# An encoder kernel with split-precision matmuls: elementwise work taken from GpSimd, and the mLSTM query prepared one group ahead

## The chip, the cores and the metric

The kernel runs on one core of a Trainium2 chip. The metric is the device time of one execution in microseconds (us): 1479.44 us, the median of 3 runs (1478.56 to 1479.59). One more execution was profiled; the views of the profile below come from it. The engines are TensorE (PE: matmuls, with PEld for the loading of the stationary operand), VectorE (DVE), ScalarE (ACT), GpSimd (POOL) and SyncE (SP), whose queue issues all the DMAs here.

## The reference

A two-layer encoder is applied to a prompt of 1024 tokens (`p`) and to a sample of 512 tokens (`s`), each with 1024 features, in float32. After each layer stands `x = layer_norm(ALPHA * x + mix)`.

Layer 0 (even) is a pool mixer beside a bidirectional mLSTM with 4 heads of 128, computed in chunks of 128 tokens:

```python
proj = x @ w_in; xa, za, xb, vb, ob, zb, gi, gf = jnp.split(proj, IN0_SPLIT_POINTS, axis=-1)
out_a = centred_pool_mixer(xa, w_pool, pool_scale) * silu(za)   # window means of 2, 4, 8, 16, minus x, then w_pool
xc = silu(centred_depthwise_conv(xb, conv_w, conv_b))           # 3 taps
q, k = xc @ w_q, xc @ w_k                                       # per head
# per chunk and direction, g = cumsum(log forget gate):
s = (q @ k.T) * exp(dmat - m_row)          # dmat causal, from the gates
num = s @ v + ex * (C @ q);  den = s.sum(-1) + ex * (n @ q)
h = num / maximum(abs(den), exp(-m_row))
C_new = decay * C + (ws * v).T @ k;  n_new = decay * n + ws @ k
out_b = (head_norm((h_fwd + h_bwd) * sigmoid(ob)) * g + skip * xc) * silu(zb)
mix = concatenate([out_a, out_b]) @ w_out
```

Layer 1 (odd) is attention with 8 query heads and 2 key heads, RMS norm and rotary tables on q and k, a softmax over the whole sequence, and a gate `silu(z)` before the output projection.

## The kernel before, in words

Every large matmul is made of three, with operands split into a high and a low part in float32r: high x high, high x low, low x high. To split a 128x512 tile takes one cast to float32r (the high part) and one subtraction (the low part). The helpers at lines 92 to 103 set the engines: `hi_pool` casts on POOL, `hi_act` on ACT, `lo_dve` subtracts on DVE, and `split_light` casts on ACT and subtracts on POOL. `mm` (line 106) issues one matmul, so most PE rows carry L106, most casts L93 or L96, most low parts L99 or L103.

The work has three stages, which the profile shows at about 0 to 155, 155 to 622, and 622 us to the end.

*First projections* (`layer0`, lines 295 to 337). For each of two pieces of 512 columns (v, then the output gate) and each of three groups of 512 tokens (p0, p1, s0), four accumulators in PSUM (`tp`, `ts`) take 24 matmuls each. ACT evacuates them into `evp` or `evs` (tag `th` of the pool `st0`, 3 buffers; lines 320 to 326) and SP stores them to DRAM. Gate columns are transposed into PSUM banks (`ctpa`, `ctpws`, `ctpex`, `ctpen`, line 507) that the accumulators before them held. Between the groups steps of `weight_sums` (line 1107) run: pieces of layer 1's weights are loaded into tiles `sr` (8 buffers), four subtractions per piece (two on POOL, two on DVE, line 1120) make sums, and these are stored for layer 1.

*Heads* (lines 338 to 404). Six periods: prompt heads 0, 1, 2 and 3 (two groups of 512 tokens each), then sample heads 0 and 1 together, and 2 and 3 together (one group each); so each period has two groups. In a period `merge` interleaves generators by their declared numbers of steps: `chains` (the passing of the state from chunk to chunk) of this period, `early` (convolution, query, scores and chunk sums) of the next, `head_fin` (norm and gating) of the one before, and projections with the pool mixer (`proj_g`, `pool_mix`) as filling. `early(s, h, ...)` (line 551) runs head by head. Per group it makes the convolution `xc` (564 to 569); splits it into `kh`, `kl`; forms q by `wqp` = three matmuls with a product of w_q and w_k, and splits it into `keep`; loads and exponentiates the gate weights `w` (ACT line 603) and masks them on POOL (606); transposes `xc` to `kt`; loads and splits v (`vh`, `vl`); multiplies `S` = k q and weights it into `ph`, `pl` (633 to 636); then twice, for two chunks each, forms `vw` = v times ws on POOL (643), splits it into `vwh`, `vwl`, multiplies `U` (the chunk sums) and `A` (the within-chunk numerators `N`). `kh`, `kl`, `vh`, `vl`, `vw`, `vwh` and `vwl` have one buffer each, q's `keep` has four. In this stage the weights of the projections (`wunit`) are split by `split_light`, since `wlight` is set. `pool_mix` makes the window sums on POOL (817) and casts its result with `hi_pool`. `out_weights` splits every second weight tile of the output projection with `split_light`.

*The rest*: the output projection and layer norm of layer 0 (part of it inside the heads' last periods, `mid_tile`, whose norm ends with two products on POOL at lines 929 and 930), then layer 1.

What sets the order: the program is emitted in the order of the generators, and a scheduler that simulates a timeline orders each engine's queue from it (`TileContext(nc, schedule_with_timeline_sim=True)`); only layer 1's PE order is written out by hand. Engines then run their queues in order. POOL also computes `rstd` as a power (line 195).

## Time and profile before

| | |
|---|---|
| median of 3 runs | 1479.44 us (1478.56 to 1479.59) |
| the profiled execution, its own time | 1477.55 us |
| its span, first to last instruction | 1475.8 us |
| instructions | 21781 |
| mean granted clock of TensorE | 0.990 |
| ACT, busy us | 738.4 (50%) |
| DMA moved, mean rate | 243.42 MB, 165 GB/s |

Engines' busy times are unions of their instructions. A matmul's recorded duration overlaps with the next one's, so matmuls are better counted by the distance of their starts. In a row of groups the fields are: line, engine, operation, tiles (output, then inputs), shapes, count, then busy us and mean ns of one, then the idle time of the engine before them and what ended it. A row of waits reads: engine and tile that waited, line, what released it, total us, times, longest. A row of the timeline or of the chain begins with start and duration in us from the span's start. The granted clock is the share of TensorE's full clock in that stretch.

### The profile page before, as it was taken

The page shows a single profiled execution, that of the slowest core. Times are in us where ns is not written, and L with a number is a line of the kernel's source. Part 1 is how long each engine was busy: PE and PEld are TensorE (multiplying, and loading weights), DVE is VectorE, ACT ScalarE, POOL GpSimd, SP SyncE. Part 2 cuts the span into 40 slices and gives each one's busy share as a digit, 9 for nine tenths or more (in the row PEclk, how much of TensorE's full clock was granted, in tenths as well). Part 3 has the DMA queues.
Part 4 walks back from the last instruction along what each step waited for, and adds up shares of the span by engine and source line. Part 5 has one row for each costly group of instructions (what it writes and reads, how often), then busy time and mean ns, then how long its engine had stood idle before and what let it go on. Part 6 is the DMA issues. An engine that isn't in the chain of part 4 may idle for free.

```text
span 1475.8 us, 21781 instructions
## 1 busy us (share of the span) xinstructions
PE 1435.2 (97%) x7190; PEld 1189.3 (81%) x7190; DVE 1012.5 (69%) x1976; ACT 738.4 (50%) x1666; POOL 609.0 (41%) x616
## 2 busy tenths in 40 slices
PE   9998999999999999999999999999999999999997
PEld 7876888878787788788888789888878888888886
DVE  6584156585777878877779548555677777777675
ACT  3341355454545555445346545557755555555551
POOL 5431334353542333659426002432345545444641
PEclk9998999999999999999999999999999999999999
DMA  9976564555597776545554876345321111111311
GB/s 311 396 282 235 190 201 139 204 176 178 160 310 245 233 229 208 181 147 185 172 167 145 271 226 234 121 136 157 114 72 58 57 51 37 43 58 58 100 51 57
DMA packets 181586, 243.42 MB, mean 165 GB/s; under 512 B 14673, under 2 KB 90193, under 8 KB 181473
## 3 DMA queue, kind: packets, MB, share of 16 engines
q1 hardware_dynamic: 181472, 242.03, 49.7%
q8 instruction: 57, 0.93, 0.3%
q14 instruction: 57, 0.46, 0.1%
HBM read 155.94 MB, written 86.03 MB: 164 GB/s over the span
## 4 chain that ended last, share of the span: by engine, by line
PE 65%; DVE 13%; DMA 12%; issue 4%; ACT 3%; POOL 2%; SPq 1%; DVEq 0%; ACTq 0%; POOLq 0%
PE Sp L106 6%; PE Op L106 6%; PE o1p L106 6%; PE ptp L1442 4%; PE o1s L106 3%; PE qs L106 3%; PE o0s L106 3%; PE z L106 3%; PE zp L106 3%; PE o0p L106 3%; PE xbp L106 2%; PE kvs L106 2%; PE ts L106 1%; PE Ss L106 1%; PE z4P L106 1%
## 5 line engine op out<-in xcount | busy, mean ns | idle before, releaser
L1420 POOL TENSOR_SCALAR prp<-prp,smp 128x1024 f32<-128x1024 f32 x64 | 73.3, 1145 | 137.8 <-DVE smp L1419 112.7
L96 ACT CAST pwp<-ptp 128x512 fp32r<-128x512 f32 x128 | 74.8, 585 | 92.1 <-PE ptp L1442 91.4
L106 PE MATMUL Op<-pwp,Vhp 128*128 128x512 f32 x256 | 109.0, 426 | 0.6 <-DVE pwp L99 0.6
L99 DVE TENSOR_TENSOR pwp<-ptp,pwp 128x512 fp32r<-128x512 f32 x128 | 87.2, 682 | 22.9 <-ACT pwp L96 22.7
L1415 ACT ACTIVATE prp<-Sp,nbp,rqp 128x1024 f32<-128x1024 f32 (+1 forms) x68 | 78.8, 1159 | 21.6 <-DVE nbp L1412 15.8
L1407 DVE TENSOR_REDUCE nbp<-Sp 128x1 f32<-128x1024 f32 (+1 forms) x68 | 78.4, 1153 | 11.8 <-PE Sp L106 11.7
L1442 PEld LDWEIGHTS ptp<-idn,prp 128*128 128x128 f32 x512 | 63.5, 140 | 20.0 <-DVE pwp L99 1.9
L1442 PE MATMUL ptp<-idn,prp 128*128 128x128 f32 x512 | 77.0, 272 | 2.0 <-POOL prp L1420 1.4
L106 PEld LDWEIGHTS Op<-pwp,Vhp 128*128 128x128 f32 x256 | 48.3, 189 | 8.0 <-DVE pwp L99 1.0
L106 PE MATMUL tp<-wt_l,xhp 128*128 128x512 f32 x128 | 51.2, 404 | 0.0
L106 PE MATMUL tp<-wt_h,xlp 128*128 128x512 f32 x128 | 51.1, 403 | 0.0
L106 PE MATMUL o0p<-wo0l,ah0p 128*128 128x512 f32 x128 | 50.8, 399 | 0.2 <-DVE wo0l L99 0.2
L106 PE MATMUL o0p<-wo0h,ah0p 128*128 128x512 f32 x128 | 50.6, 397 | 0.2 <-ACT wo0h L96 0.2
L106 PE MATMUL tp<-wt_h,xhp 128*128 128x512 f32 x128 | 50.7, 403 | 0.0
L106 PE MATMUL o0p<-wo0h,al0p 128*128 128x512 f32 x128 | 50.3, 394 | 0.0
L106 PE MATMUL Op<-pwp,Vlp 128*128 128x512 f32 x128 | 50.1, 391 | 0.0
L1067 POOL TENSOR_TENSOR rskp<-sskp,mhalf 128x2 f32<-128x2 f32 x8 | 7.0, 879 | 100.2 <-DVE sskp L1063 100.2
L106 PE MATMUL Sp<-Khp,qhp 128*128 128x512 f32 x128 | 41.9, 403 | 0.0
L106 PE MATMUL o1p<-wo,ah1p 128*128 128x512 f32 x128 | 40.7, 399 | 0.0
L106 PE MATMUL Sp<-Klp,qhp 128*128 128x512 f32 x128 | 40.7, 393 | 0.0
L106 PE MATMUL Sp<-Khp,qlp 128*128 128x512 f32 x128 | 40.4, 391 | 0.0
L699 DVE SCALAR_TENSOR_TENSOR Usp<-Usp,decbp 128x130 f32<-128x130 f32 x48 | 22.2, 462 | 25.8 <-ACT Usp L656 25.2
(1150 smaller groups left out, 4999.5 us busy)
## 6 DMA issues: line engine op xcount, KB each, us to landing
wt_r<-w0t SPq DMA_DIRECT2D x16, 256.0 KB, 5.2
xrp<-xT_p SPq DMA_DIRECT2D x16, 256.0 KB, 5.4
srq<-w1q SPq DMA_DIRECT2D x16, 256.0 KB, 5.4
sum_q<-srq SPq DMA_DIRECT2D x16, 256.0 KB, 5.3
srz<-w1z SPq DMA_DIRECT2D x16, 256.0 KB, 5.1
sum_z<-srz SPq DMA_DIRECT2D x16, 256.0 KB, 4.8
wp<-rd_p SPq DMA_DIRECT2D x16, 256.0 KB, 4.9
z_p<-zsp SPq DMA_DIRECT2D x16, 256.0 KB, 3.2
```

Source lines behind the costliest of these rows:

```text
L96: self.nc.scalar.copy(out, in_)
L99: self.nc.vector.tensor_tensor(out=out, in0=in_, in1=hi.bitcast(F32), op=ALU.subtract)
L106: self.nc.tensor.matmul(out, lhsT=lhsT, rhs=rhs, start=start, stop=stop)
L699: nc.vector.scalar_tensor_tensor(out=U[:, i, :], in0=U[:, i + o, :], scalar=dec[:, 4 * d + h, n:n + 1], in1=U[:, i, :], op0=ALU.mult, op1= ...
L1067: nc.gpsimd.tensor_tensor(out=rs[:, 0:nh], in0=ss[:, 0:nh], in1=self.mhalf[:, 0:nh], op=ALU.pow)
L1407: nc.vector.tensor_reduce(out=nb[:, i:i + 1], in_=b, op=ALU.max, axis=AX.X, negate=True)
L1415: nc.scalar.activation(pr[:, i * W:(i + 1) * W], b, AF.Exp, bias=nb[:, 0:1], scale=rq, accum_out=sm[:, i:i + 1])
L1420: nc.gpsimd.tensor_scalar(pr, pr, sm, 0.0, ALU.mult, ALU.add)
L1442: nc.tensor.transpose(pt[:, h * P:(h + 1) * P], prs[h][:, c * P:(c + 1) * P], self.idn)
```

## The change

- The evacuation tiles `th` of the first projections get 4 buffers, the tiles `sr` of the weight sums 7 instead of 8; all four subtractions of a piece run on DVE.
- In the heads `wunit` casts on ACT and subtracts on DVE (`hi_w = hi_act`, and `wlight` is never set). `out_weights` does so for all its tiles. The casts of `kh`, `vh` and of the pool mixer go from POOL to ACT; the window sums and the products `vw` go from POOL to DVE. POOL keeps the masks (606), the powers (195), memsets and the layer norm's two products.
- `early` takes all heads of a period as one stream: all convolutions first, then `query` (the split of k, q and its split) for the first group, and for each group, once S is done, `query` of the next group ahead of U and A. The tiles N and keep are taken in `query`. The product `vw` for the first two chunks is made ahead of the step's end at S, the one for the other two right after the first U. The stream is declared with 8 steps a group instead of 10.

The diff, cut to its core:

```diff
@@ -317,7 +317,7 @@
-                            t = st.tile([P, 512], F32, tag="th", name=f"ev{s}{piece}{n}")
+                            t = st.tile([P, 512], F32, tag="th", name=f"ev{s}{piece}{n}", bufs=4)
@@ -343,7 +343,7 @@
-            self.wlight = True
+            self.hi_w = self.hi_act
@@ -388,8 +388,8 @@
-                    jobs.append((chain(*[self.early(*hd, hp, hf) for hd in periods[i + 1]]),
-                                 total(lambda s: 10 * self.seqs[s][0] // 512, periods[i + 1])))
+                    jobs.append((self.early(periods[i + 1], hp, hf),
+                                 total(lambda s: 8 * self.seqs[s][0] // 512, periods[i + 1])))
@@ -401,7 +401,7 @@
-            self.wlight = False
+            self.hi_w = self.hi_pool
@@ -548,51 +548,72 @@
-    def early(self, s, h, hp, hf):
-        nc = self.nc
-        xbs = self.xbt.pop((s, h))
-        NG = self.seqs[s][0] // 512
-        col = self.cols[s]
-        hc = slice(h * P, (h + 1) * P)
-        xcs, vs = [], []
-        for g in range(NG):
-            gc = slice(g * 512, (g + 1) * 512)
-            xb = xbs[g]
+    def early(self, heads, hp, hf):
+        nc = self.nc
+        items = []
+        for s, h in heads:
+            xbs = self.xbt.pop((s, h))
+            U = self.chain_tile(s, h, hf)
+            self.state[s, h] = (U, [], [])
+            items += [(s, h, g, xb, U) for g, xb in enumerate(xbs)]
+        xcs, qs, vws = [], {}, {}
+        for s, h, g, xb, _ in items:
...
-            self.load(self.xcd[s][h, :, gc], xc)
+            self.load(self.xcd[s][h, :, g * 512:(g + 1) * 512], xc)
...
+        def query(n):
+            s, h, g, _, _ = items[n]
+            kh = hf.tile([P, 512], F32R, tag="kh", name=f"kh{s}{h}{g}")
+            kl = hp.tile([P, 512], F32R, tag="kl", name=f"kl{s}{h}{g}")
...
-            vs.append((N, keep))
-        U = self.chain_tile(s, h, hf)
-        q, Ns = [], []
-        for g in range(NG):
-            gc, ns = slice(g * 512, (g + 1) * 512), slice(4 * g, 4 * g + 4)
-            xc = xcs[g]
-            kh = hf.tile([P, 512], F32R, tag="kh", name=f"kh{s}{h}{g}")
-            kl = hp.tile([P, 512], F32R, tag="kl", name=f"kl{s}{h}{g}")
-            N, keep = vs[g]
...
-            self.hi_pool(kh, xc)
-            self.lo_dve(kl, xc, kh)
+            self.state[s, h][1].append((qh, ql))
+            self.state[s, h][2].append(N)
+            qs[n] = kh, kl, qh, ql, N
+            self.hi_act(kh, xcs[n])
+            self.lo_dve(kl, xcs[n], kh)
...
+            hc = slice(h * P, (h + 1) * P)
...
-            q.append((qh, ql))
-            yield
+            yield
+        def weighted(n, i, v):
+            s, h, g, _, _ = items[n]
+            vw = hf.tile([P, 2, 2, 130], F32, tag="vw", name=f"vw{s}{h}{g}{i}")
+            vb = v[:, i:i + 2, :].unsqueeze(2).to_broadcast([P, 2, 2, 130])
+            ws = self.cols[s]["ws"][:, 4 * g + i:4 * g + i + 2, :, h:h + 1].to_broadcast([P, 2, 2, 130])
+            nc.vector.tensor_tensor(out=vw, in0=vb, in1=ws, op=ALU.mult)
+            vwh = hf.tile([P, 2, 2, 130], F32R, tag="vwh", name=f"vwh{s}{h}{g}{i}")
+            vwl = hf.tile([P, 2, 2, 130], F32R, tag="vwl", name=f"vwl{s}{h}{g}{i}")
+            self.hi_act(vwh, vw)
+            self.lo_dve(vwl, vw, vwh)
+            return vwh, vwl
+        yield from query(0)
+        for n, (s, h, g, _, U) in enumerate(items):
+            gc, ns = slice(g * 512, (g + 1) * 512), slice(4 * g, 4 * g + 4)
+            hc = slice(h * P, (h + 1) * P)
+            xc, col = xcs[n], self.cols[s]
+            kh, kl, qh, ql, N = qs.pop(n)
@@ -619,7 +640,7 @@
-            self.hi_pool(vh, v)
+            self.hi_act(vh, v)
@@ -634,26 +655,22 @@
-            yield
+            vws = weighted(n, 0, v)
+            yield
+            if n + 1 < len(items):
+                yield from query(n + 1)
...
-                vw = hf.tile([P, 2, 2, 130], F32, tag="vw", name=f"vw{s}{h}{g}{i}")
-                vb = v[:, i:i + 2, :].unsqueeze(2).to_broadcast([P, 2, 2, 130])
-                ws = col["ws"][:, 4 * g + i:4 * g + i + 2, :, h:h + 1].to_broadcast([P, 2, 2, 130])
-                nc.gpsimd.tensor_tensor(out=vw, in0=vb, in1=ws, op=ALU.mult)
-                vwh = hf.tile([P, 2, 2, 130], F32R, tag="vwh", name=f"vwh{s}{h}{g}{i}")
-                vwl = hf.tile([P, 2, 2, 130], F32R, tag="vwl", name=f"vwl{s}{h}{g}{i}")
-                self.hi_act(vwh, vw)
-                self.lo_dve(vwl, vw, vwh)
-                yield
+                vwh, vwl = vws
...
-                    n = 4 * g + i + j
-                    kc = slice((n % 4) * P, (n % 4 + 1) * P)
-                    pu = self.bank("mc", f"U{s}{h}{n}", (P, 2, 130))
+                    m = 4 * g + i + j
+                    kc = slice((m % 4) * P, (m % 4 + 1) * P)
+                    pu = self.bank("mc", f"U{s}{h}{m}", (P, 2, 130))
...
-                    nc.scalar.copy(U[:, 2 * n:2 * n + 2, :], pu)
+                    nc.scalar.copy(U[:, 2 * m:2 * m + 2, :], pu)
+                if i == 0:
+                    vws = weighted(n, 2, v)
@@ -663,8 +680,6 @@
-            Ns.append(N)
-        self.state[s, h] = (U, q, Ns)
@@ -814,7 +829,7 @@
-                nc.gpsimd.tensor_tensor(out=nxt[:, 0:ln], in0=cur[:, 0:ln], in1=cur[:, step:step + ln], op=ALU.add)
+                nc.vector.tensor_tensor(out=nxt[:, 0:ln], in0=cur[:, 0:ln], in1=cur[:, step:step + ln], op=ALU.add)
@@ -826,7 +841,7 @@
-            self.hi_pool(qh, cur[:, 0:512])
+            self.hi_act(qh, cur[:, 0:512])
@@ -859,11 +874,8 @@
-            if k % 2:
-                self.split_light(h, l, raw)
-            else:
-                self.hi_act(h, raw)
-                self.lo_dve(l, raw, h)
+            self.hi_act(h, raw)
+            self.lo_dve(l, raw, h)
@@ -1113,22 +1125,22 @@
-                    t = r[h, j] = pool.tile([P, 512], F32, tag="sr", name=f"sr{kind}{k}{h}{j}", bufs=8)
+                    t = r[h, j] = pool.tile([P, 512], F32, tag="sr", name=f"sr{kind}{k}{h}{j}", bufs=7)
...
-                for o, e, x, y, d in ((0, nc.gpsimd, (0, 1), (0, 0), (0, 0)), (2, nc.vector, (1, 1), (0, 1), (0, 1)),
-                                      (1, nc.gpsimd, (1, 1), (0, 0), (1, 1)), (3, nc.vector, (1, 1), (1, 0), (1, 0))):
-                    e.tensor_tensor(out=r[d], in0=r[x], in1=r[y], op=ALU.subtract)
+                for o, x, y, d in ((0, (0, 1), (0, 0), (0, 0)), (2, (1, 1), (0, 1), (0, 1)),
+                                   (1, (1, 1), (0, 0), (1, 1)), (3, (1, 1), (1, 0), (1, 0))):
+                    nc.vector.tensor_tensor(out=r[d], in0=r[x], in1=r[y], op=ALU.subtract)
```

More of the change, by code (lines that the diff above doesn't have):

```diff
@@ L1115, in weight_sums @@
                 for h, j in ((0, 0), (0, 1), (1, 1), (1, 0)):
-                    t = r[h, j] = pool.tile([P, 512], F32, tag="sr", name=f"sr{kind}{k}{h}{j}", bufs=8)
+                    t = r[h, j] = pool.tile([P, 512], F32, tag="sr", name=f"sr{kind}{k}{h}{j}", bufs=7)
                     self.load(t.rearrange("p (k n) -> p k n", k=2) if kind == "kv" else t, self.piece(kind, k, h, j))
-                for o, e, x, y, d in ((0, nc.gpsimd, (0, 1), (0, 0), (0, 0)), (2, nc.vector, (1, 1), (0, 1), (0, 1)),
-                                      (1, nc.gpsimd, (1, 1), (0, 0), (1, 1)), (3, nc.vector, (1, 1), (1, 0), (1, 0))):
-                    e.tensor_tensor(out=r[d], in0=r[x], in1=r[y], op=ALU.subtract)
+                for o, x, y, d in ((0, (0, 1), (0, 0), (0, 0)), (2, (1, 1), (0, 1), (0, 1)),
+                                   (1, (1, 1), (0, 0), (1, 1)), (3, (1, 1), (1, 0), (1, 0))):
+                    nc.vector.tensor_tensor(out=r[d], in0=r[x], in1=r[y], op=ALU.subtract)
                     self.load(self.sums[kind][k, o], r[d])
                 yield
-        g = pool.tile([P, 4, P], F32, tag="sr", name="srg", bufs=8)
+        g = pool.tile([P, 4, P], F32, tag="sr", name="srg", bufs=7)
         self.load(g.rearrange("p a f -> p (a f)"), self.a["g4"].partition_broadcast(P))
@@ L1127, in weight_sums @@
             for i, n in enumerate(("cos", "sin")):
-                t = pool.tile([P, 4, P], F32, tag="sr", name=f"srt{h}{n}", bufs=8)
+                t = pool.tile([P, 4, P], F32, tag="sr", name=f"srt{h}{n}", bufs=7)
                 self.load(t, self.a[n][:, ns, :])
                 for w in range(2):
-                    o = pool.tile([P, 4, P], F32, tag="sr", name=f"sro{h}{n}{w}", bufs=8) if w == 0 else t
+                    o = pool.tile([P, 4, P], F32, tag="sr", name=f"sro{h}{n}{w}", bufs=7) if w == 0 else t
                     nc.vector.tensor_tensor(out=o, in0=t, in1=g[:, 2 * w + i:2 * w + i + 1, :].to_broadcast([P, 4, P]), op=ALU.mult)
```

## The prediction

> **What bounds the kernel now.** I read the page first, then the busy time by stage and in 40 us slices, then the chain and the engine timelines around the slices where TensorE's granted clock is below 1, then the groups by shape.
>
> ```profile
> span 1475.8 us, 21781 instructions
> ## 1 busy us (share of the span) xinstructions
> PE 1435.2 (97%) x7190; PEld 1189.3 (81%) x7190; DVE 1012.5 (69%) x1976; ACT 738.4 (50%) x1666; POOL 609.0 (41%) x616
> ```
>
> TensorE (PE) is busy 97% of the span, and the change leaves every matmul in place. So it can win only what PE idles or runs at a reduced clock, and can lose only by making PE wait. The three stages (first projections, heads, the rest) show where that is:
>
> ```profile
> 0.00:155.00 155.00, 145.22 (x641) 117.10 (x642) 90.81 (x117) 47.42 (x86) 56.95 (x65) 0.97 0.82 297
> 155.00:622.00 467.00, 448.49 (x2313) 376.65 (x2312) 329.72 (x713) 232.55 (x561) 191.93 (x222) 0.99 0.63 205
> 622.00:1476.00 854.00, 841.47 (x4238) 695.56 (x4237) 592.01 (x1146) 458.41 (x1020) 360.08 (x330) 1.00 0.37 119
> ```
>
> The columns after the width are busy us (and count) of PE, PEld, DVE, ACT, POOL, then granted clock, DMA share, GB/s. PE is idle 9.8 us in the first stage and 18.5 us in the heads (467.00 - 448.49). The rest of the program is not touched and I leave it as it is. In slices of 40 us:
>
> ```profile
> 120.00:160.00 40.00, 33.32 (x166) 27.01 (x165) 9.19 (x12) 7.88 (x27) 6.58 (x6) 0.87 0.67 244
> 280.00:320.00 40.00, 39.59 (x219) 33.99 (x218) 33.49 (x71) 23.35 (x58) 20.97 (x23) 1.00 0.40 134
> 320.00:360.00 40.00, 36.79 (x182) 31.29 (x183) 22.06 (x49) 19.81 (x52) 10.98 (x15) 0.91 0.62 205
> 360.00:400.00 40.00, 38.26 (x190) 31.70 (x190) 32.10 (x71) 19.71 (x50) 23.24 (x26) 1.00 0.47 152
> 480.00:520.00 40.00, 37.26 (x189) 31.71 (x190) 33.21 (x83) 22.80 (x55) 15.85 (x24) 0.91 0.78 243
> 560.00:600.00 40.00, 39.52 (x198) 32.41 (x198) 34.96 (x92) 18.03 (x43) 18.68 (x15) 1.00 0.64 203
> ```
>
> The clock column dips in the three slices that hold the longest waits of PE, and a dip costs about as much again as its wait: 0.09 x 40 = 3.6 us of clock in each of 320 to 360 and 480 to 520, of which I count 3.0 as time in which PE had work. These are the waits, the first from the first stage, the others from the heads:
>
> ```profile
> PE ctpen L507 <- ACT evp L325: 6.7, 1, 6.7
> ...
> PE Up L106 <- DVE vwlp L99: 2.8, 1, 2.8
> PE Ss L106 <- DVE keeps L99: 2.2, 1, 2.2
> PE hTs L772 <- ACT ths L768: 2.2, 1, 2.2
> PE Sp L106 <- ACT keepp L96: 1.5, 1, 1.5
> PE Bp L106 <- DVE clp L99: 1.3, 2, 0.8
> PE zs L106 <- DVE zss L541: 1.2, 1, 1.2
> PE Ap L106 <- ACT Np L664: 1.1, 2, 0.9
> ```
>
> Everything to be won: 6.7 + 18.5 us of waiting, and three dips of about 3 us.
>
> **Part 1, four evacuation buffers in the first stage.** ScalarE's timeline, then the queue that stores:
>
> ```profile
> 119.61 2.00 ACT L325 ACTIVATE evp<-tp 128x512 f32<-128x512 f32 x3 [0.98 <-PE tp L106]
> 132.34 0.60 ACT L325 ACTIVATE evp<-tp 128x512 f32<-128x512 f32 x1 [10.74 <-DMA thd_p<-evp]
> ...
> 126.63 2.29 SPq L90 DMA_DIRECT2D thd_p<-evp  x3
> ```
>
> Three of four accumulators leave PSUM at once; the fourth needs a `th` buffer and waits 10.7 us for the first store, which the SP queue issued only at 126.6. Its bank is the one that the transposes of `ctpen` want, hence the 6.7 us. With bufs=4 the fourth copy follows the third and is done at about 122.3, before `ctpen` begins to wait (132.9 - 6.7 = 126.2). No store is late for it: its slot was last used by the piece before, whose stores had let the first three go at once. After the wait PE runs slowly for a while, as the chain shows:
>
> ```profile
> 134.07 10.03 PE tp L106 x32
> 144.09 8.19 PE ts L106 x36
> 153.40 13.84 PE ts L106 x60
> ```
>
> 32 matmuls at 313 ns instead of the 229 ns of the next 96: 2.7 us. Gone together: 9.4 us. Next late is the first weight block of the heads:
>
> ```profile
> 154.28 2.54 POOL L103 TENSOR_TENSOR xbp0u_l<-xbp0u_r,xbp0u_h 128x512 fp32r<-128x512 f32 x2 [28.97 <-ACT xbp0u_h L96]
> 167.06 0.39 PE L106 MATMUL xbp<-xhp,xbp0u_h 128*128 128x512 f32 x1
> ```
>
> Its split ends at 156.8 and PE takes it at 167.1, so PE may come 9.4 us earlier and still find it, with under 1 us to spare. Bounds: 0 (something else delays the bank) to -9.8.
>
> **Part 2, from POOL to VectorE and ScalarE.** These are the prices:
>
> ```profile
> L699 DVE SCALAR_TENSOR_TENSOR Usp<-Usp,decbp 128x130 f32<-128x130 f32 x48 | 22.2, 462 | 25.8 <-ACT Usp L656 25.2
> L727 DVE SCALAR_TENSOR_TENSOR Np<-Bp,colpex,Np 128x130 f32<-128x130 f32 x56 | 17.3, 344 | 7.2 <-PE Bp L106 7.2
> ...
> L99 DVE TENSOR_TENSOR vwlp<-vwp,vwhp 128x520 fp32r<-128x520 f32 x16 | 11.0, 690 | 0.6 <-ACT vwhp L96 0.5
> ```
>
> ```profile
> L643 POOL TENSOR_TENSOR vwp<-vrp,colpws 128x520 f32<-128x520 f32 x16 | 18.9, 1183 | 20.9 <-DVE vwlp L99 18.1 <-DMA act_p<-xcrp 1.5 <-PE xbp L106 1.3
> ...
> L195 POOL TENSOR_TENSOR r0p_rs<-r0p_ve,mhalf 128x4 f32<-128x4 f32 x8 | 8.3, 1033 | 22.5 <-DVE r0p_ve L193 22.3
> ...
> L93 POOL TENSOR_SCALAR khp<-xcp 128x512 fp32r<-128x512 f32 x8 | 7.0, 871 | 9.2 <-PE Sp L106 4.0 <-DVE abp L744 3.2 <-DVE xcp L568 2.0
> L93 POOL TENSOR_SCALAR vhp<-vrp 128x520 fp32r<-128x520 f32 x8 | 6.4, 805 | 5.0 <-PE Ap L106 3.9 <-DMA vrp<-vd_p 1.1
> ```
>
> DVE gets 40 low halves (32 of input weights, 8 of output weights), 24 products `vw` and 30 window sums: 94 instructions at 690 ns, 65 us. It also gets something back. L699 and L727 are the same operation on the same shape; L727 reads one operand from PSUM and takes 344 ns, L699 reads both from SBUF and takes 462 in the mean, stretched where it runs beside POOL. Each DVE instruction of the heads' 713 against the shortest quarter of its own line and shape: 64 us too long in all, 51 of it beside POOL work that this change removes, the rest beside what stays (masks, the layer norm's products). Net: DVE goes from 330 to about 344 us of 467. The powers (L195) also have two SBUF operands and stay on POOL; the 30 DVE instructions that ran beside one lost 0.1 us together, so I charge nothing for them. The page "SBUF — State Buffer" of the Trainium skill, section "Who interferes with whom", says that a DVE instruction with two SBUF inputs and a GpSimd instruction that reads SBUF exclude each other, the later one waiting for the whole of the other: by it L699 would be explained, but the eleven powers of the heads would hold DVE up for as much as 11 us more, and 14 would become 25; the trace does not show that.
>
> ACT gets 36 casts (12 each for kh, vh and the pool mixer) at the 0.60 us of the evacuation row: 22 us, from 233 to 255 of 467, which fits. But two waits come along: the kh and vh casts have one buffer each and wait for S and A of the group before, on POOL 4.0 and 3.9 us in all by the rows. On ACT the exponentials and the copies U and N out of PSUM are queued behind them, and PE waits for those copies (the Ap row, 1.1). I charge 1 us, at most 8. No DMA is added in the heads, and none passes another on SP's queue.
>
> Cost on PE of the 14 us more on DVE: now 18.5 us of PE waiting go with 330 us of DVE work, 6%, so 0.8 us; at most the 14 itself. I take 3, as a new wait may bring a dip of its own.
>
> In the first stage 20 weight sums go from POOL to DVE (14 us at 690 ns) and lengthen 90.8 to at most 105 of 155; the weights' casts that share POOL with them there get room. I take 0, between -2 and +4. One buffer fewer in `sr` (7 for 8) still holds a piece of four and three of the next: 0 to +2.
>
> **Part 3, q one group ahead, vw before the yield.** Each period has two groups (two chunks of a prompt head, or two sample heads), so q runs ahead for the second of each pair only. The 2.2 us of Ss, which end at 481 us, are such a second group's: they go, with its dip, 5.2 us. The 1.5 us of Sp is the first group of all and stays. The 2.8 us of Up is the second half of a group, whose vw chain now starts before the first half's A products, with a product of 690 ns for POOL's 1183; it goes with the 0.9 us of Ap behind it and the dip, 6.7 us. Half of Bp and of the small waits on POOL's casts: 1.5 us. hTs (2.2) belongs to the layer-norm products that stay. Sum -13.4; bounds 0 and -24.5 (18.5 and two dips).
>
> **The sum.** -9.4 - 13.4 + 1 + 3 = -18.8 us. The profiled execution took 1477.55 us (1475.8 of span and 1.75 around it), so 1458.8; the median of the runs is 1.9 above it, so 1460.7. I forecast 1460.5, with 1453 to 1467 as the case's own range.
>
> **Rivals.** (a) All of the heads' waits go, since they came from DVE work stretched by POOL: 1479.4 - 9.4 - 24.5 = 1445.5. For it: L699's row, and that most of the waits are on DVE; against: hTs and Sp. Chance 0.11. (b) The heads come out even, new waits for DVE's fuller queue taking the place of the old, and only the buffer counts: 1470. For it: the whole order of the queues is planned anew, and DVE stays at 74%. Chance 0.19. (c) Even that buffer brings nothing, since the bank or the stores behind it hold PE at the same place: 1479. Chance 0.07.
>
> (d) Slower: DVE becomes the bound of the heads. In four of the twelve slices (280, 360, 480, 560) it is busy 32.1 to 35.0 of 40 already, and with a twelfth of the 65 us in each, 37.5 to 40.4. If the 51 us do not come back, because kept POOL reads and DVE's own queue eat them, a third of them falls in slices without room: +17 - 9.4 = +7.6, that is 1487. It decides from about 85% of DVE busy over the heads (395 of 467). Against it: the two rows above. The page "Perfetto Trace Analysis" of the Trainium skill, section "Optimizing Scalar/DVE Operations", speaks for this rival: where DVE is saturated, work may be better on Scalar or even GpSimd; it adds that moves between DVE and GpSimd may not help. Chance 0.14.
>
> **Numbers.** Forecast 0.49, (a) 0.11, (b) 0.19, (c) 0.07, (d) 0.14. The measurement tells 0.2% (3 us) from no change. Faster: 0.49 + 0.11 + 0.19, less 0.02 for the edge of (b), 0.77; same that 0.02 and 0.06 of (c), 0.08; slower 0.15. Range 1445 to 1483: down to (a), up past (c) into the low end of (d); some 0.17 is outside.
>
> **What would show it.** Right: no wait of `ctpen`; granted clock 1.00 in 120 to 160; L699 near 345 ns; DVE near 345 us and PE idle near 10 us in the heads; no wait of Ss on keeps. Wrong: DVE over 390 us there, or new PE waits of over 2 us on DVE or on U and N copies with the clock down behind them.

## The result and the profile after

The kernel after takes 1462.61 us (median of 3 runs, 1460.97 to 1465.09) against 1479.44 before: a ratio of 0.9886, interval 0.9867 to 0.9906, or 16.8 us less. The forecast was 1460.5. The profiled execution of after is the slowest of its three, 1465.09 us with a span of 1463.3; before's, at 1477.55, lies below its median. So the two profiles stand only 12.5 us apart in span, and what follows accounts for those 12.5. Each profile is one execution, and executions of one kernel differ by some us, so a difference of a few us in one stage of two profiles is a hint and not a measurement.

The head of the page of after:

```profile
span 1463.3 us, 21759 instructions
## 1 busy us (share of the span) xinstructions
PE 1432.1 (98%) x7190; PEld 1190.3 (81%) x7190; DVE 1021.8 (70%) x2090; ACT 753.7 (52%) x1702; POOL 434.9 (30%) x466
```

TensorE (PE) does the same 7190 matmuls. POOL lost 174 us of work, VectorE (DVE) gained only 9, although 114 instructions moved to it: it has got time back. By the fixed windows of the prediction (columns as there: width, then busy us and count of PE, PEld, DVE, ACT, POOL, then PE's granted clock, DMA share, GB/s):

```profile
0.00:155.00 155.00, 153.21 (x689) 124.50 (x690) 95.95 (x139) 46.18 (x86) 24.00 (x46) 1.00 0.86 306
155.00:622.00 467.00, 453.14 (x2344) 382.96 (x2344) 342.40 (x823) 255.17 (x609) 59.82 (x96) 0.98 0.65 208
```

PE's idle time fell from 9.8 to 1.8 us in the first stage and from 18.5 to 13.9 in the heads. DVE is busy 342.4 us of 467 there, where the sum said 344.

Fixed windows cut two kernels at different work once one of them runs ahead. A better cut is at work itself: the first matmul into `xbp` (start of the heads), into `qP1i` (start of layer 1) and into `z0P`. The stage called heads is longer by this cut: it also holds the output projection and the norm of layer 0. The stretch from `qP1i` to `z0P` is called the entry of layer 1. Both kernels issue the same number of matmuls up to each of these. Before, cut at 167.1, 711.3 and 793.2:

```profile
0.00:167.10 167.10, 157.32 (x695) 127.09 (x696) 90.81 (x117) 50.32 (x91) 61.44 (x70) 0.97 0.82 295
167.10:711.30 544.20, 525.55 (x2681) 440.33 (x2680) 396.12 (x853) 272.34 (x650) 253.49 (x279) 0.99 0.60 197
711.30:793.20 81.90, 81.90 (x373) 66.63 (x372) 63.94 (x113) 40.18 (x133) 30.70 (x25) 1.00 0.51 161
793.20:1475.80 682.60, 670.40 (x3445) 555.25 (x3443) 461.66 (x896) 375.54 (x793) 263.33 (x243) 1.00 0.34 108
```

And after, cut at 157.1, 693.9 and 778.3:

```profile
0.00:157.10 157.10, 154.55 (x695) 125.25 (x695) 97.11 (x141) 47.97 (x90) 24.00 (x46) 1.00 0.85 304
157.10:693.90 536.80, 523.70 (x2680) 441.92 (x2681) 396.74 (x941) 288.51 (x684) 111.44 (x149) 0.98 0.63 202
693.90:778.30 84.40, 82.49 (x373) 66.51 (x373) 66.10 (x115) 41.83 (x136) 36.33 (x30) 1.00 0.52 166
778.30:1463.30 685.00, 671.40 (x3445) 556.58 (x3444) 461.86 (x896) 375.44 (x793) 263.12 (x243) 0.99 0.34 107
```

Read the widths: the first stage is 10.0 us shorter, the heads 7.4 shorter, the entry of layer 1 is 2.5 longer and the rest 2.4 longer. PE was never idle at the entry before (81.90 busy of 81.90). The sum is -12.5. The forecast's terms were -9.4 for the first stage, -9.4 for the heads (-13.4 + 1 + 3), and nothing behind them.

PE's longest waits after:

```profile
PE zp L106 <- ACT xbpp L524: 2.4, 1, 2.4
PE Up L106 <- ACT vwhp L96: 2.3, 1, 2.3
PE hTs L787 <- ACT ths L783: 2.2, 1, 2.2
PE Bp L106 <- ACT Uss L671: 2.0, 1, 2.0
PE x1t L981 <- DMA y<-x_s: 1.8, 1, 1.8
...
PE As L106 <- DVE keeps L99: 1.7, 1, 1.7
...
PE qP6i L106 <- DVE u L1183: 1.2, 1, 1.2
```

The wait of `ctpen` is gone. Those of the heads are not: four are of 2 us or more where there were three, and the four longest now all end on ScalarE (ACT), where two of the three longest had ended on DVE. And the clock still dips in the heads (their granted clock is 0.98 after and 0.99 before), as two slices of after show:

```profile
120.00:160.00 40.00, 39.23 (x182) 31.75 (x181) 17.02 (x29) 8.61 (x29) 0.10 (x1) 1.00 0.85 297
...
440.00:480.00 40.00, 35.44 (x172) 29.41 (x171) 30.16 (x78) 24.13 (x57) 3.51 (x8) 0.87 0.69 216
```

The first dip, at 120 to 160, is gone as foretold; a new one of 0.87 stands at 440 to 480. Last, the two groups that priced the stretching on DVE, after the change (busy us and mean ns stand behind the bar):

```profile
L742 DVE SCALAR_TENSOR_TENSOR Np<-Bp,colpex,Np 128x130 f32<-128x130 f32 x56 | 17.4, 345 | 3.7 <-PE Bp L106 3.7
L714 DVE SCALAR_TENSOR_TENSOR Usp<-Usp,decbp 128x130 f32<-128x130 f32 x48 | 17.1, 357 | 13.3 <-ACT Usp L671 13.0
```

L714 is before's L699: 462 ns has become 357.

### The profile page after: what moved, and what is told of

Its sections match the earlier page's. It is cut to its first block, busy times and chain, and to the rows that moved or that the text cites. A ratio compares the mean times of both kernels' runs of the same rounds, so it can differ in the third digit from the quotient of the medians.

```text
span 1463.3 us, 21759 instructions
## 1 busy us (share of the span) xinstructions
PE 1432.1 (98%) x7190; PEld 1190.3 (81%) x7190; DVE 1021.8 (70%) x2090; ACT 753.7 (52%) x1702; POOL 434.9 (30%) x466
## 4 chain that ended last, share of the span: by engine, by line
PE 71%; DVE 10%; DMA 8%; issue 4%; POOL 3%; ACT 3%; SPq 1%; DVEq 0%; ACTq 0%; POOLq 0%
PE Sp L106 6%; PE o1p L106 6%; PE Op L106 6%; PE zp L106 5%; PE ptp L1454 4%; PE tp L106 3%; PE o1s L106 3%; PE qs L106 3%; PE zs L106 3%; PE z L106 3%; PE xap L106 2%; PE xbp L106 2%; PE o0p L106 2%; PE Ss L106 2%; PE kvs L106 2%
## 5 line engine op out<-in xcount | busy, mean ns | idle before, releaser
L627 POOL TENSOR_SCALAR_AFFINE_SELECT wp<-wp 128x512 f32<-128x512 f32 x16 | 10.8, 675 | 144.0 <-ACT wp L624 112.0
L624 ACT ACTIVATE wp<-wp,colpa 128x128 f32<-128x128 f32 x64 | 21.0, 394 | 31.9 <-DMA wp<-rd_p 30.6
```

Source lines behind the costliest of these rows:

```text
L624: nc.scalar.activation(w[:, d, c], w[:, d, c], AF.Exp, bias=col["a"][:, 4 * g + i, d, h:h + 1])
L627: nc.gpsimd.affine_select(out=wv, in_=wv, pattern=[[0, 4], [sg, P]], compare_op=ALU.is_ge, fill=0.0, base=0, channel_multiplier=-sg)
```

## The experiments

Two questions were open. Does the first stage's gain come from the buffer (the prediction's reason) or from the weight sums leaving POOL? And does the heads' gain come from the new order of the stream (the prediction's reason) or from the move of work off POOL (which the prediction priced as a cost)? Each run does one part alone, or undoes one part. The table gives every run with its median, its ratio to the kernel before on the same chip, and the widths of the four stages in its own profile, cut as above. The ratios rest on 3 to 12 executions of a kernel, the widths on one. That one can lie well off the median: e9's took 1477.93 us (median 1473.95), e2's 1470.10 (1464.63), e10's 1460.25 (1463.66). So the ratios decide, and the widths say where to look.

| run | us | ratio (interval) | first | heads | entry | rest |
|---|---|---|---|---|---|---|
| before | 1479.44 | 1 | 167.1 | 544.2 | 81.9 | 682.6 |
| after | 1462.61 | 0.9886 (0.9867-0.9906) | 157.1 | 536.8 | 84.4 | 685.0 |
| e1 | 1476.08 | 0.9972 (0.9958-0.9987) | 165.0 | 543.7 | 82.3 | 682.4 |
| e2 | 1464.63 | 0.9900 (0.9878-0.9922) | 158.9 | 538.4 | 88.7 | 682.4 |
| e3 | 1478.68 | 0.9990 (0.9978-1.0001) | 167.2 | 540.7 | 84.1 | 683.9 |
| e4 | 1460.91 | 0.9869 (0.9849-0.9889) | 159.9 | 534.0 | 82.9 | 684.6 |
| e5 | 1473.00 | 0.9957 (0.9943-0.9970) | 160.3 | 542.5 | 82.4 | 682.9 |
| e6 | 1472.27 | 0.9955 (0.9939-0.9971) | 166.5 | 534.9 | 88.4 | 682.1 |
| e7 | 1473.48 | 0.9962 (0.9944-0.9979) | 157.0 | 537.7 | 93.1 | 682.9 |
| e8 | 1456.58 | 0.9848 (0.9835-0.9860) | 156.6 | 529.2 | 87.0 | 681.0 |
| e9 | 1473.95 | 0.9971 (0.9958-0.9985) | 167.1 | 534.5 | 92.4 | 682.2 |
| e10 | 1463.66 | 0.9894 (0.9879-0.9909) | 166.5 | 526.5 | 83.8 | 681.7 |
| e11 | 1462.68 | 0.9891 (0.9877-0.9906) | 157.1 | 535.0 | 87.9 | 682.3 |
| e12 | 1459.98 | 0.9869 (0.9852-0.9886) | 157.5 | 530.4 | 84.5 | 684.5 |

**e1, the buffer alone.** The kernel before, with this edit:

```diff
-                            t = st.tile([P, 512], F32, tag="th", name=f"ev{s}{piece}{n}")
+                            t = st.tile([P, 512], F32, tag="th", name=f"ev{s}{piece}{n}", bufs=4)
...
-                    t = r[h, j] = pool.tile([P, 512], F32, tag="sr", name=f"sr{kind}{k}{h}{j}", bufs=8)
+                    t = r[h, j] = pool.tile([P, 512], F32, tag="sr", name=f"sr{kind}{k}{h}{j}", bufs=7)
```

> The kernel before with four evacuation tiles th (and seven sr tiles, so that both fit), and nothing else. My theory: the 6.7 us wait of ctpen and the slow clock behind it go, 9.4 us, and nothing else moves: 1470 us (1468 to 1473), the first heads' matmul xbp near 157.5 us instead of 167.1. Rival one, the buffer is the whole gain and the heads only came out even: 1463. Rival two, the store or the bank still holds PE there: 1479.

The heads begin 2.1 us earlier, not 9.4. PE's longest wait moved from `ctpen` to the transposes just ahead of it:

```profile
PE ctpex L507 <- ACT evp L325: 6.3, 1, 6.3
```

ACT's timeline in e1 (start, duration, instruction, idle time before it and its releaser) says why:

```profile
109.24 1.30 ACT L325 ACTIVATE evp<-tp 128x512 f32<-128x512 f32 x2 [0.40 <-PE tp L106]
123.38 0.20 ACT L489 ACTIVATE decs<-decs 40x4 f32<-40x4 f32 x1 [12.84 <-DVE decs L488]
123.50 1.05 ACT L325 ACTIVATE evp<-tp 128x512 f32<-128x512 f32 x2
```

All four buffers are there, yet two accumulators stay in PSUM for 13 us: their copies stand in ACT's queue behind `decs`, and `decs` waits for DVE's chain of gate sums. In DVE's timeline of e1 two neighbours of that chain show what slows it:

```profile
113.50 2.30 DVE L469 TENSOR_TENSOR_SCAN ms<-LFs,GIs 8x512 f32<-8x512 f32 x1
115.83 1.21 DVE L470 TENSOR_TENSOR_SCAN ms<-LFs,GIs 8x512 f32<-8x512 f32 x1
```

The same scan takes 2.30 us while POOL subtracts weights, from 112.20 to 114.72 in POOL's timeline, and 1.21 right behind it.

This is not what held the bank before. There `decs` was done ahead of the copies, and the first three of them waited for PE alone, as the prediction's row at 119.61 shows:

```profile
118.43 0.21 ACT L489 ACTIVATE decs<-decs 40x4 f32<-40x4 f32 x1 [7.48 <-DVE decs L488]
```

The buffer did take its own wait away. But the queues were planned anew with it: the transposes now come 8 us earlier (`ctpa` at 116.6 for 124.6), `decs` comes 5 us later, and two copies stand behind it. One wait went, and the new order made another.

**e5, the weight sums alone.** The kernel before, with the two POOL subtractions of each set on DVE:

```diff
-                for o, e, x, y, d in ((0, nc.gpsimd, (0, 1), (0, 0), (0, 0)), (2, nc.vector, (1, 1), (0, 1), (0, 1)),
-                                      (1, nc.gpsimd, (1, 1), (0, 0), (1, 1)), (3, nc.vector, (1, 1), (1, 0), (1, 0))):
+                for o, e, x, y, d in ((0, nc.vector, (0, 1), (0, 0), (0, 0)), (2, nc.vector, (1, 1), (0, 1), (0, 1)),
+                                      (1, nc.vector, (1, 1), (0, 0), (1, 1)), (3, nc.vector, (1, 1), (1, 0), (1, 0))):
```

> The kernel before with the weight sums' four subtractions all on DVE, and nothing else (three th tiles, heads as before). What the runs so far suggest: the first stage's wait went in both kernels that had the sums on DVE, with three buffers too. My theory now: the sums on DVE, not the buffer, take that wait away, since neither POOL nor DVE's gate chain is held up any more and the stores behind the sums leave earlier: 1471 (1469 to 1474), xbp near 159 us instead of 167.1, no wait of ctpen over 1 us. Rival: the wait went because the whole plan of the queues came out another way with the heads' moves: 1477 or more, ctpen still waiting 6 us.

The heads begin 6.8 us earlier, with three buffers as before. The fourth copy still waits for its buffer, as ACT's timeline of e5 shows, but the transposes no longer wait for it: in PE's list of waits `ctpen` and `ctpex` do not appear.

```profile
130.50 0.60 ACT L325 ACTIVATE evp<-tp 128x512 f32<-128x512 f32 x1 [8.49 <-DMA thd_p<-evp]
```

The missing buffer costs PE something at the end of the stage instead: the first matmul of the heads waits for the last copy of the sample's group, which waits for a store.

```profile
159.68 0.60 ACT L325 ACTIVATE evs<-ts 128x512 f32<-128x512 f32 x1 [4.01 <-DMA thd_s<-evs]
...
PE xbp L106 <- ACT evs L325: 4.7, 1, 4.7
```

That wait is 0.8 us in after, with four buffers. One observation goes beyond a single plan: in all six kernels with half of the sums on POOL (before, e1, e3, e6, e9, e10) one of these transposes waits 6.3 to 6.9 us, and in all eight with all sums on DVE none does. So in these plans the sums decide whether that wait is there. How they do it is less sure, for in e5 PE's queue is planned in another order too: 11 matmuls stand between `ctpex` and `ctpen`.

DVE itself became faster. The groups of subtractions on DVE, for z in the kernel before and in e5:

```profile
L1120 DVE TENSOR_TENSOR srz<-srz,srz 128x512 f32<-128x512 f32 x8 | 6.9, 861 | 2.6 <-POOL srz L1120 2.6
```

```profile
L1120 DVE TENSOR_TENSOR srz<-srz,srz 128x512 f32<-128x512 f32 x16 | 10.9, 684 | 0.2
```

861 ns has become 684, and the waiting for POOL's half is gone, so twice the work costs DVE only 4.0 us more (10.9 for 6.9), of which 2.4 come back as idle time saved.

**e4, after without its buffer.** The kernel after with `th` at three and `sr` at eight:

```diff
-                            t = st.tile([P, 512], F32, tag="th", name=f"ev{s}{piece}{n}", bufs=4)
+                            t = st.tile([P, 512], F32, tag="th", name=f"ev{s}{piece}{n}")
```

> The changed kernel with three th tiles and eight sr tiles again. My theory: ctpen waits again for the fourth evacuation, 9 us, all of it seen at the end: 1472 (1469 to 1475). Rival: later waits (weights, stores) swallow part of it, so that the buffer is worth under 5 us here: 1463 to 1467.

The heads begin 2.8 us later than in after and are 2.8 us shorter: both reach layer 1 at 693.9. In whole time the intervals of e4 and after overlap. Once the sums are on DVE, the fourth buffer gains in the first stage and nothing that can be told from 0 at the end.

**e3, the new stream alone.** The kernel before with the new `early` (q of the next group ahead, vw before the yield, 8 steps declared), every operation kept on its old engine:

```diff
-                    jobs.append((chain(*[self.early(*hd, hp, hf) for hd in periods[i + 1]]),
-                                 total(lambda s: 10 * self.seqs[s][0] // 512, periods[i + 1])))
+                    jobs.append((self.early(periods[i + 1], hp, hf),
+                                 total(lambda s: 8 * self.seqs[s][0] // 512, periods[i + 1])))
...
+            if n + 1 < len(items):
+                yield from query(n + 1)
```

> The kernel before with the new early (one stream, q one group ahead, vw before the step's end) and all engines as before, POOL making kh, vh, vw and the window sums; three th tiles. My theory: the wait of the second groups' S on keep goes, and Up's on vwl, about 4 to 8 us: 1473 (1470 to 1477), with L699 still near 460 ns. Rival one, without the engines' move the order alone gains nothing, since DVE work is stretched as before: 1479 (1477 to 1482). Rival two, the order is the whole of the heads' gain: 1471 or less.

Nothing that can be measured: the interval holds 1, and a gain of over 0.22% (3 us) is outside it. The heads are 3.5 us shorter, and 3.5 us go again in the entry (+2.2) and the rest (+1.3). PE's waits in e3:

```profile
PE hTs L787 <- ACT ths L783: 3.4, 1, 3.4
PE As L106 <- DVE keeps L99: 3.1, 1, 3.1
PE Ap L106 <- DVE mvp L776: 2.1, 1, 2.1
```

The wait for `keep` was to go. It only moved, from the scores (Ss 2.2) to the products A (As 3.1). A does not read `keep`; by the code, A takes its PSUM bank from the same three (`me`) as the product q, and such a bank comes free only when q has been split.

**e7, after with q not ahead.** One line moved, so that q is made right before its own scores:

```diff
-        yield from query(0)
...
+            yield from query(n)
...
-            if n + 1 < len(items):
-                yield from query(n + 1)
```

> The changed kernel with q made right ahead of its own group's scores, as before the change, and all else as changed. My theory after the runs so far, in which the new order alone gained 1 us: 1463 (1460 to 1465), PE waiting on keep for at most 2 us more. Rival, the step of my prediction: the wait of a second group's S on keep and a dip of the clock come back, 5 us: 1468.

In whole time it is 11 us slower than after, which looks like the worth of q ahead. The stages put it elsewhere: layer 1 is reached at 694.7 against 693.9, so 0.8 us were lost by then, and the entry of layer 1 alone is 8.7 us longer. PE's waits between 694 and 789 us in e7:

```profile
PE qP6i L106 <- DVE u L1181: 3.0, 1, 3.0
PE qP2i L106 <- DVE w1q5l L99: 2.7, 1, 2.7
```

Neither is a wait for q: the weights of layer 1 (`w1q5l`) are split, and its input `u` is made, too late by DVE. The two may still hang together, since DVE did 4.5 us less in the heads than in after (392.2 for 396.7) and 4.4 more at the entry (70.5 for 66.1): work was put off. Whether q's place caused this, or only the new plan that comes with any edit, is not shown.

**e2, all moves between engines, without stream and buffer.** The kernel before with every operation on the engine that after gives it:

```diff
-            self.hi_pool(kh, xc)
+            self.hi_act(kh, xc)
...
-                nc.gpsimd.tensor_tensor(out=vw, in0=vb, in1=ws, op=ALU.mult)
+                nc.vector.tensor_tensor(out=vw, in0=vb, in1=ws, op=ALU.mult)
...
-                nc.gpsimd.tensor_tensor(out=nxt[:, 0:ln], in0=cur[:, 0:ln], in1=cur[:, step:step + ln], op=ALU.add)
+                nc.vector.tensor_tensor(out=nxt[:, 0:ln], in0=cur[:, 0:ln], in1=cur[:, step:step + ln], op=ALU.add)
```

and in the same way the `vh` and pool mixer casts, the odd output-weight blocks, the low halves of the input weights and the weight sums.

> The kernel before with every POOL operation of the change moved (casts to ACT, low halves, vw, window sums and weight sums to DVE), three th tiles and the old order of early. My theory: L699 falls from 462 to about 350 ns and DVE stays near 345 us busy in the heads; the ctpen wait stays; the heads win about 4 us, as only part of the waits came from stretched DVE work: 1475 (1471 to 1479). Rival one, the stretched DVE work was behind all of the heads' gain: 1471 or less. Rival two, DVE becomes the bound: 1482 or more, with PE waits on DVE over 2 us.

This is most of the change: 0.9900, with an interval that overlaps that of after. The next three runs take it apart.

**e6, those moves in the heads only.** As e2, with the weight sums left on POOL; of its edit against the kernel before, the lines that set it apart from e10 below:

```diff
-            self.hi_pool(kh, xc)
+            self.hi_act(kh, xc)
...
-            self.hi_pool(vh, v)
+            self.hi_act(vh, v)
...
-            self.hi_pool(qh, cur[:, 0:512])
+            self.hi_act(qh, cur[:, 0:512])
```

> The kernel before with the heads' moves from POOL to ACT and DVE alone; weight sums, th and the order of early as before. My theory: the heads (from the first xbp to the first qP1i) shorten from 544 to about 538 us, as in the kernel with all engine moves, and the first stage stays: 1473 (1471 to 1476), xbp near 167. Rival: the heads' moves gain nothing by themselves, the 15 us of all moves being the sums' alone: 1479 (1477 to 1482).

The heads are 9.3 us shorter and L699 takes 356 ns, but the entry gives 6.5 us back, and the whole comes to 0.9955. With e5's 0.9957 the two parts make 0.9912 (0.9955 + 0.9957 - 1), near e2's 0.9900.

**e9, the casts alone.** The kernel before with just these lines of e6, 36 casts (kh, vh, pool mixer) on ACT, and everything else on its old engine:

```diff
-            self.hi_pool(kh, xc)
+            self.hi_act(kh, xc)
...
-            self.hi_pool(qh, cur[:, 0:512])
+            self.hi_act(qh, cur[:, 0:512])
```

> The kernel before with only the 36 one-operand casts (kh, vh, the pool mixer's high part) moved from POOL to ACT; all two-operand work stays on POOL. My theory, that the heads gain from DVE work no longer stretched by POOL's two-operand work: L699 stays near 460 ns, the heads (first xbp to first qP1i, 544.2 us before) stay within 2 us, the time 1478 (1476 to 1481). Rival, that a slow and queued POOL held up kh, vh and the mixer's part, and PE behind them: the heads shorten by 5 us or more, 1473.

The rival of this expectation came out, in the time and in the heads, and not the theory: the heads become 9.7 us shorter, although DVE is stretched nearly as before. Its group of U in e9:

```profile
L699 DVE SCALAR_TENSOR_TENSOR Usp<-Usp,decbp 128x130 f32<-128x130 f32 x48 | 24.6, 514 | 24.1 <-ACT Usp L656 23.8
```

So the heads can shorten while VectorE's instructions stay long. Less than half of it lasts: by the ratio the kernel is 4 us faster than before, and its profiled execution is no faster. The heads and the entry of e9, cut at its own 167.1, 701.6 and 794.0:

```profile
167.10:701.60 534.50, 520.90 (x2681) 438.04 (x2680) 380.27 (x842) 286.20 (x680) 220.63 (x238) 0.99 0.61 198
701.60:794.00 92.40, 85.34 (x373) 67.13 (x372) 71.35 (x123) 43.46 (x139) 35.56 (x31) 0.98 0.49 157
```

The entry takes 92.4 us for the same 373 matmuls, 10.5 more than before, waiting for splits of layer 1's weights and for `u`. Against before DVE did 15.8 us less in the heads (396.12 to 380.27) and 7.4 more at the entry (63.94 to 71.35), so part of its work was put off.

**e10, the two-operand work alone.** The kernel before with the low halves of the weights, the products vw and the window sums on DVE, and the odd output-weight blocks on ACT and DVE; the 36 casts and the weight sums stay on POOL:

```diff
-            self.wlight = True
+            self.hi_w = self.hi_act
...
-                nc.gpsimd.tensor_tensor(out=vw, in0=vb, in1=ws, op=ALU.mult)
+                nc.vector.tensor_tensor(out=vw, in0=vb, in1=ws, op=ALU.mult)
...
-                nc.gpsimd.tensor_tensor(out=nxt[:, 0:ln], in0=cur[:, 0:ln], in1=cur[:, step:step + ln], op=ALU.add)
+                nc.vector.tensor_tensor(out=nxt[:, 0:ln], in0=cur[:, 0:ln], in1=cur[:, step:step + ln], op=ALU.add)
...
-            if k % 2:
-                self.split_light(h, l, raw)
-            else:
-                self.hi_act(h, raw)
-                self.lo_dve(l, raw, h)
+            self.hi_act(h, raw)
+            self.lo_dve(l, raw, h)
```

> The kernel before with only the two-operand work (low parts, vw, window sums) moved from POOL to DVE and the casts left on POOL. My theory: this carries the heads' gain; L699 near 355 ns, the heads 7 to 10 us shorter, 1473 (1470 to 1476). Rival, that the casts' place matters as much: half of it, heads 3 to 5 us shorter, 1476 or more.

This part alone equals the whole change in time (0.9894 against 0.9886, intervals overlapping), with the first stage untouched. Its heads and its group of U:

```profile
166.50:693.00 526.50, 518.95 (x2682) 438.67 (x2681) 402.01 (x941) 271.19 (x647) 139.17 (x186) 0.99 0.62 202
```

```profile
L699 DVE SCALAR_TENSOR_TENSOR Usp<-Usp,decbp 128x130 f32<-128x130 f32 x48 | 18.6, 387 | 9.6 <-ACT Usp L656 9.4
```

The heads are 17.7 us shorter, the best of all, and little of it is given back: the entry is 83.8, 1.9 longer. DVE has 88 instructions more than before there and is busy only 5.9 us longer (402.01 against 396.12). PE's waits in e10's heads are few; the longest is 2.2.

**e8, the layer norm's products too.** The kernel after with the last large two-operand work that POOL has in the heads moved to DVE (the powers of 128x4 stay):

```diff
-            nc.gpsimd.tensor_tensor(out=xr[:, c], in0=xr[:, c], in1=g, op=ALU.mult)
-            nc.gpsimd.tensor_tensor(out=xr[:, c], in0=xr[:, c], in1=b, op=ALU.add)
+            nc.vector.tensor_tensor(out=xr[:, c], in0=xr[:, c], in1=g, op=ALU.mult)
+            nc.vector.tensor_tensor(out=xr[:, c], in0=xr[:, c], in1=b, op=ALU.add)
```

> The changed kernel with the two products of layer 0's norm on DVE instead of POOL, for every token tile that takes that path. My theory: DVE loses the last 10 us of stretching in the heads, gets 16 us of products there, and the wait of hTs (2.2 us), which I put down to those products on POOL, goes: 1461 (1458 to 1463). Rival one: hTs waits as long as before, since DVE's own queue holds it: 1463 to 1465. Rival two: DVE is full where the products come, and PE waits there: 1467 or more.

It is the fastest kernel here, 1456.58 us, with an interval wholly below that of after. The heads and the entry of e8:

```profile
156.60:685.80 529.20, 519.92 (x2681) 440.66 (x2682) 402.30 (x972) 286.49 (x678) 55.48 (x106) 0.99 0.62 204
685.80:772.80 87.00, 84.15 (x373) 67.67 (x372) 68.91 (x130) 44.88 (x143) 34.81 (x28) 0.98 0.51 164
```

The heads are another 7.6 us shorter than in after, and the wait of hTs, which the prediction laid to these products, is on its list of waits no more. That they caused it is not shown: in e10, where they stay on POOL, hTs waits only 0.5 us. DVE took 31 more instructions in the heads for 5.6 us.

**e11, the plan shaken.** The kernel after with 10 steps declared for the stream instead of 8, which alters only the planned order:

```diff
-                                 total(lambda s: 8 * self.seqs[s][0] // 512, periods[i + 1])))
+                                 total(lambda s: 10 * self.seqs[s][0] // 512, periods[i + 1])))
```

> The changed kernel with early declared at 10 steps a group instead of 8: the same instructions, interleaved a little otherwise, so that the queues are planned anew. My theory: what a new plan alone does is some 3 us at the end, 1462 (1459 to 1466), with the same first stage to 1 us. Rival: plans alone move the time by as much as the change's parts, 8 us or more, 1470, and then the parts' sizes can't be read from whole times.

The whole time is that of after. The stages shift by -1.8 (heads), +3.5 (entry) and -2.7 (rest): shifts of that size in one stage, from a new order or from one execution to the next, carry no reading.

**e12, one step further.** e8 with the rotary addition (L1087) on DVE as well:

```diff
-        nc.gpsimd.tensor_tensor(out=t1[:, 0:W], in0=t1[:, 0:W], in1=t2[:, 0:W], op=ALU.add)
+        nc.vector.tensor_tensor(out=t1[:, 0:W], in0=t1[:, 0:W], in1=t2[:, 0:W], op=ALU.add)
```

> The changed kernel with the norm's two products on DVE, as in the run that was the fastest so far, and the addition of the rotary step in layer 1 moved from POOL to DVE as well. My theory, that POOL's two-operand work stretches DVE there too (16 of 48 instructions beside it, 14 us, in the trace of that run): the wait of the transposes Tqp on the addition (2.3 us) goes, 1454 (1451 to 1456). Rival: DVE is the fuller engine there and nothing is gained, 1457 to 1460.

No gain over e8 (0.9869 against 0.9848, intervals just overlapping). In e8 the transposes Tqp waited for the rotary addition on POOL, in e12 they wait as long for DVE. First e8's list, then e12's:

```profile
PE Tqp L1247 <- POOL t0qp L1087: 2.3, 2, 2.0
```

```profile
PE Tqp L1247 <- DVE ssqp L1078: 2.1, 1, 2.1
```

## Why the prediction was right in size, and wrong in most of its reasons

The time came out 2 us above the forecast, and each of its two large terms lies near a gain that some stage shows. But the reasons under those terms fell, one after the other. That the number was right is luck: the gain of the sums, priced at 0, stood in for the buffer's, and the gain of the moves off POOL, priced as a cost, stood in for the stream's.

**Part 1, the buffer, -9.4.** The first stage did become 10.0 us shorter, the wait of `ctpen` went and the clock of 120 to 160 is 1.00. The step that failed is that the buffer alone does it, with the weight sums taken at 0. Its reading of the kernel before was right. But it held that with the buffer "the fourth copy follows the third" in an order that is otherwise kept, and asked only whether a store would be late. In e1 the order changed and two copies stand in ACT's queue behind `decs`; the buffer alone brings 2.1 us in the stage. The sums, priced at 0 with -2 as the best end, bring 6.8 (e5). The prediction looked at how much DVE work they add (14 us of 155) and not at what they free: DVE waits no more for POOL's half, and its gate chain is no longer stretched beside it. That the chain's lengthening is what made PE wait is argued, not shown, since the order changed with the sums as well. Rival (c) came nearest to e1: a bank holds PE for 6.3 us there, though one transpose earlier.

**Part 2, engines, priced at +4.** The terms of the sum were right: DVE 342.4 us for 344 foretold, L714 at 357 ns for "near 345". Against the shortest quarter of each line and shape, DVE's instructions of the heads were 64 us too long before and 14.5 after, 9.6 of them beside the layer norm's products that stayed. The failed step is the last one, "cost on PE of the 14 us more on DVE". It multiplied a total by an average share of waiting, as if DVE mattered by how long it is busy. e10 shows the reverse sign: with DVE 5.9 us busier the heads are 17.7 us shorter. This move, by itself, is worth the whole gain.

Why it is worth so much is only in part shown. One reading is that of rival (a): PE waits for a certain DVE result at a certain moment, and a result that took 462 ns in the mean comes out at 387 or 357. The other is that results which POOL made (a product `vw` in 1183 ns) come earlier from a queue with less in it. The runs do not separate the two, and the first is not enough. By the measure above the stretching is 55 us in e9, 17 in e6, 21.5 in e10 and 5.5 in e8, against 64 before, and the heads are shorter by 9.7, 9.3, 17.7 and 15.0: e9 gains as much as e6 with three times its stretching. Nor did all of the heads' waits go, as (a) said: PE still idles 13.9 us there after.

The casts were charged 1 us, at most 8. e6 and e10 differ in them alone (and in the plan): 534.9 against 526.5 us in the heads, 1472.27 against 1463.66 in all. So on top of the two-operand work they cost 8.6 us, past the far end of the range, and four of the five longest waits in after's heads end on ACT. Alone they shorten the heads (e9). Why they do the one here and the other there is not settled: a trace shows waits for ACT behind them and splits put off, but no run separates the cast's place on ACT from the order that the planner makes of it. A kernel after with its casts left on POOL was not tried.

**Part 3, the stream, -13.4.** This is the step that failed outright. Alone it brings nothing (e3). The waits that were to go moved one product further: keeps from Ss to As (1.7 after, 3.1 in e3), and Up waits 2.3 us for the high half of vw where it had waited 2.8 for the low. The wait of Ss on keeps is also gone in e9 and e10, which have the old stream. Without q ahead the kernel after is 11 us slower (e7), clear of the intervals, but only 0.8 us of it by the end of the heads; the rest is lost at the entry, for a reason that stays open. On top of the engine moves the stream is worth a little: e4 is e2 with the new stream, and stands at 0.9869 to 0.9900, 3.7 us in medians, with intervals that just overlap.

**"The rest of the program is not touched."** Its instructions are not, but their order is, and it lost 4.9 us in the profiles (2.5 at the entry, 2.4 behind it). e7 and e9 lose 11.2 and 10.5 at the entry against before, e2 and e6 6.8 and 6.5. Nothing in those edits touches layer 1's instructions at the entry; e11, which changes only a number of steps, has an entry 3.5 us longer than after's.

**Part by part,** in ratios times 1479.4: sums -6.4 (e5), two-operand work -15.7 (e10), casts +9.0 (e6 less e10), sums and heads' moves together another -1.8 (e2), stream -4.6 (e4 less e2), buffer +2.5 (after less e4, not told apart from 0): together -16.9 before rounding. The interval of each ratio reaches 2 to 3 us to either side, so the small terms are rough.

**Rival (d) and the pages.** DVE as the bound of the heads would show at about 85% busy; it is at 73% after (342.4 of 467) and 74% in e8. The page "Perfetto Trace Analysis" of the Trainium skill, section "Optimizing Scalar/DVE Operations", holds that work of a saturated DVE may be better on ScalarE or even GpSimd, and adds that moves between GpSimd and DVE might not help, as the two share an SBUF read port. DVE was not saturated here (71% busy in the heads before), and this case's rows agree with the second half: to have 88 instructions of the heads on POOL had spared DVE only 5.9 us (e10). In e12 the moves stop paying, with a wait for DVE in place of one for POOL. And the powers: 23 DVE instructions of the heads ran beside one of 128x4 in after and lost 0.14 us together. The page "SBUF — State Buffer" of the Trainium skill states in "SBUF: two separate sides" that the engine that starts first gets the shared ports for the whole instruction; by that the powers would have cost up to 11 us, an estimate from that page; the trace does not show it for instructions of that size.

## What to carry to other kernels

Here the operations on POOL that read two SBUF operands were paid for on VectorE (64 us of stretching in the heads before, 14.5 after): price the removal of such work by what VectorE's instructions get back and by which results TensorE then gets earlier, and not by VectorE's total. Before crediting a buffer with a wait, ask which order the planner will make once the buffer is there, and what then stands ahead of the waiting copy in its engine's queue. And where every edit plans the queues anew, look at the moment at which a stage's first matmul starts to see where a part acts, and at whole times of several executions to see what it is worth.

## What the runs showed that was not expected

Casts with one SBUF operand on POOL stretch VectorE as well: with the sums gone (e5), 9 of the 25 DVE instructions beside a 128x512 cast of the first stage ran long against the shortest quarter of their line and shape, 3.6 us together; all nine are 128x512 subtractions of two SBUF operands. PE's clock dips behind waits that are short: in after's slice of 440 to 480, which stands at 0.87, the longest waits are the 2.0 us of Bp and the 1.7 of As. Last, a stage whose instructions nobody edited can lose 11 us: the entry of layer 1 took from 81.9 us (before) to 93.1 (e7) for the same 373 matmuls, and e7's whole time, 11 us above after's, agrees.
